# A written order for the loads at the entry of attention, and a fixed order for the first row norms, in a two-layer encoder on one Trainium2 core

## The chip, the cores and the metric

The kernel runs on one core of one Trainium2 chip. The metric is the device time of one execution in microseconds (us). The engines are named as in the profile: PE (TensorE, the matrix engine; PEld is its weight load), DVE (VectorE), ACT (ScalarE), POOL (GpSimd) and SP (SyncE, which here only issues loads and stores). SPq, ACTq and POOLq are the sequencers that issue for an engine.

## What is computed

Two layers of an encoder on x of 1024 rows by 1024 columns, all float32. The reference, cut to what matters here:

```python
for l in range(2):
    h = rms_norm(x, g_norm[l])
    z = h @ w_in[l]                      # 2656 columns: q, k, v, gate of A, B, C
    # A: 6 heads, 2 key heads, per-head norm of q and k, axial rotary, full attention
    oa = dense_gqa_blocks(qa, ka, va, HEAD_DIM ** -0.5) * silu(ag)
    # B: 6 heads, 2 key heads, window of 128, a sink logit per head
    ob = windowed_sink_gqa(qb, kb, vb, b_sink, HEAD_DIM ** -0.5) * silu(bg)
    # C: 4 heads, low-rank q and kv, a shared rotary key
    oc = mla_blocks(qc_nope, qc_rope, kc_nope, kc_rope, vc, 96 ** -0.5) * silu(cg)
    x = x + concat([oa, ob, oc], -1) @ w_out[l]
return rms_norm(x, final_g)
```

## The kernel before

Rows come in NS = 8 tiles of 128. A product of float32 accuracy is made of three matmuls on values split in a high and a low part (`mm3`: high by high, high by low, low by high), so nearly everything has an `h` and an `l` twin: `wh`/`wl` of a weight piece, `hTh`/`hTl` of the transposed normed rows.

A layer goes through these stages. **Norm and v** (layer 0): for each row tile x is loaded (`load_x`, up to XBUFS tiles ahead), normed (`stage.norm`: squares on ACT, `ms_x` on DVE, a power on POOL for `rs_x`, the product `xt` on DVE), transposed by PE (`stage.turn`, `pt`) and multiplied with the v columns (`v_rows`, `pzv`). The v weights are two pieces `wst_1`, `wst_2`, split by POOL (`wh`) and DVE (`wl`) as every weight piece after them. **q and k of A, B and C** (`pza`, `pzb`, `pzc`): the results are normed, rotated, split and written to DRAM (`d_qa`, `d_ka`, `d_qb`, `d_kb`, `d_qc`, `d_kn`, `d_k`, `d_vc`). **Gate** (`pg`): PE computes the gate columns, ACT makes `g` of each result, and each is written to DRAM (`d_gate`, 256 KB a write) by ACT's own queue; all other loads and stores are issued by SP. **Attention** sweeps eight query tiles `qt`. For each, A's units take scores `sa` from keys `ka` and stacked queries `qsta`, B's take `sb` from `kb` and `qstb`, C's take `sc` from `k` and `qc`; the softmaxed scores are transposed (`ppa`, `ppb`, `ppc`) and multiplied with v (`poa`, `pob`, `poc`; C's v is `vC`). `gta`, `gtb`, `gtc` are the gate values read back for a query tile. **Output** (`pw`): the result times w_out, plus x; in the last layer with the final norm.

The keys are two halves of precision: `ka` and `kb` are two tiles each (high and low), each loaded by two loads of 512 KB; a stack of queries is four loads of 96 KB. C's keys `k` are six loads (three of 512 KB, three of 256 KB), its queries `qc` of one query tile 15 loads of 64 KB or less, `vC` one load of 1 MB.

Two things set the order. A scheduler, which sees data, buffers and priorities, orders the instructions of each engine when the kernel is built; `tc.keep_in_program_order` pins an instruction to the order in which the code says it (class `Engine` does so for all engines while `pinned[0]` is set). And each engine takes its instructions strictly in that order, so an instruction that waits holds all behind it, on SP too. Each load or store signals its end on one of eight completion counters, DMAHW0 to DMAHW7, which SP's and ACT's loads and stores take in turn; a load or store waits until the one that had its counter last has ended. The waits that the order listing below shows at loads are these.

Of the kernel before, what the change touches and what calls it, by code (L numbers as in the profile page):

```python
# [8 lines left out]
F32 = mybir.dt.float32  # L9
F32R = mybir.dt.float32r  # L10
AF = mybir.ActivationFunctionType
ALU = mybir.AluOpType
# [4 lines left out]
EPS = 1e-6  # L17
# [17 lines left out]
XBUFS = 6  # L35
# [10 lines left out]
def kernel(  # L46
# [21 lines left out]
    nc = tc.nc  # L68
    P = 128
    S, D = x.shape[1], x.shape[2]  # L70
    DEPTH = norm_g.shape[0]
    NS = S // P
# [6 lines left out]
    dram = ctx.enter_context(tc.tile_pool(name="dram", bufs=1, space=DRAM))  # L79

    queue_behind = [None]
    last_pow = [None]

    def after(ins, first):
# [9 lines left out]
    def dma(dst, src, eng=None):  # L94

        a, b = (t.bitcast(F32) if t.dtype == F32R else t for t in (dst, src))
        ins = (eng or nc.sync).dma_start(a, b)  # L97
        if queue_behind[0] is not None and eng is None:
            after(ins.ins, queue_behind[0])
        return ins.ins  # L100

    pinned = [False]
# [123 lines left out]
    for l in range(DEPTH):  # L226
# [18 lines left out]
        with stage.ph as ph:  # L245
# [32 lines left out]
            if l == 0:  # L278
                stage.open_px()
                warm = ps_o("warm")  # L280
                for _ in range(WARM):
                    T.matmul(warm[:, 0:P], lhsT=ident, rhs=ident, start=True, stop=True)
                xts = {}

                def load_x(st):
                    xts[st] = stage.px.tile([P, D], F32, tag="xt", name=f"xt{l}_{st}", bufs=XBUFS)
                    queue_behind[0] = dma(xts[st], x_src[st * P : (st + 1) * P, :])

                load_x(0)
                dma(stage.ng, norm_g[l].partition_broadcast(P))  # L290
                stage.load_wv()
                for st in range(1, XBUFS):
                    load_x(st)
                for st in range(NS):
                    xt = xts[st]
                    junk = stage.px.tile([P, D], F32, tag="junk", name=f"jk{l}_{st}", bufs=1)
                    stage.norm(st, xt, xt, junk)
                    stage.turn(st, xt, ps_t)
                    if st + XBUFS < NS:
                        load_x(st + XBUFS)  # L300
                    if st:
                        v_rows(st - 1)
                v_rows(NS - 1)
                stage.px_.close()
            else:
                for st in range(NS):
                    v_rows(st)
                    if st == LATE:
                        stage.turn(NS - 1, stage.xt, ps_t)
                stage.px_.close()  # L310
# [344 lines left out]
        with ExitStack() as ph:  # L655
# [195 lines left out]


            if True:
                ks, start = {}, {}
                for g, m0 in (("a", 0), ("b", 3)):
                    start[g] = Gqa(g, 0, m0)
# [272 lines left out]
            def groups_c():  # L1129
                for hp in range(2):  # L1130
                    ks = KeysC(hp)
                    for q0 in range(0, NS, 3):
                        c = GroupC(ks, hp, q0)
                        if hp or q0:
                            c.gate()
                        else:

                            for it in (start["a"], start["b"], c):
                                it.gate()
                            yield None  # L1140
                        for par in range(2):
                            grp = {}
                            yield [UnitC(c, par, g, grp) for g in range(c.nq)]

            def units():

                cs = groups_c()
                next(cs)
                for qt in range(NS):
                    if qt == 0:  # L1150
                        a, b = start["a"], start["b"]
                    else:
                        a, b = Gqa("a", qt, 0), Gqa("b", qt, 3)
                        a.gate()
                        b.gate()
                    for kv in range(2):
                        grp = {}
                        for g in range(3):
                            yield UnitA(a, kv, g, grp)
                            if g == 1:  # L1160
                                yield UnitB(b, kv)
                        if 2 * qt + kv in C_AT:
                            yield from next(cs)
                first = True
                for us in cs:
                    for u in us:
                        yield u
                        if first:
                            yield ab_done
                            first = False  # L1170
# [8 lines left out]
        with ExitStack() as ph:  # L1179
# [10 lines left out]
            for st in range(NS):  # L1190
                nm = f"{l}_{st}"
                s_ = slice(st * P, (st + 1) * P)
                if st > 1:
                    x_row(st)
                    out_hl(0, 6, st)
                if st:
                    out_hl(6, 8, st)
                y = xrows[st]
                if last:
                    ss = small.tile([P, 2], F32, tag="ss2", name=f"ssf{nm}")  # L1200
                for c in range(2):
                    cs = slice(c * 512, (c + 1) * 512)
                    for _ in out_part(st, c, MW if (st, c) in wa_.ps else 0, 8):
                        pass
                    ps = wa_.ps[st, c]
                    V.tensor_add(y[:, cs], ps, y[:, cs])
                    if last:
                        jk = wb.tile([P, 512], F32, tag="jk", name=f"jkf{nm}_{c}", bufs=2)
                        A.activation(jk, y[:, cs], AF.Square, accum_out=ss[:, c : c + 1])
                if last:  # L1210
                    V.tensor_add(ss[:, 0:1], ss[:, 0:1], ss[:, 1:2])
                    r = rstd_of(ss[:, 0:1], D, f"f{nm}", 1)
                    for c in range(2):
                        cs = slice(c * 512, (c + 1) * 512)
                        V.tensor_mul(y[:, cs], y[:, cs], fg[:, cs])
                    A.activation(y[:, 0:512], y[:, 0:512], AF.Copy, scale=r[:, 0:1])
                    dma(x_dst[s_, 0:512], y[:, 0:512], nc.scalar)
                    V.tensor_scalar(y[:, 512:1024], y[:, 512:1024], r[:, 0:1], None, ALU.mult)
                    dma(x_dst[s_, 512:1024], y[:, 512:1024])
                    continue  # L1220
                dma(x_dst[s_, :], y)
                if not last:
                    xt = stage.px.tile([P, D], F32, tag="xt", name=f"xt{l + 1}_{st}", bufs=XTB)
                    stage.norm(st, xt, y, xt)
                    if st == WV_ST:
                        stage.load_wv()
                    if st < NS - 1:
                        stage.turn(st, xt, ps_t)
                    else:
                        stage.xt = xt  # L1230
# [72 lines left out]
```

## Time and profile before

| | |
|---|---|
| time, median of 3 runs | 1340.75 us (1340.05 to 1341.09) |
| the profiled execution, its own time | 1342.18 us |
| its span in the trace | 1340.4 us, mean granted clock of PE 0.988 |
| PE busy | 1301.9 us, 97% of the span |
| PEld, DVE, ACT, POOL busy | 85%, 67%, 54%, 39% |
| read and written in DRAM | 107.35 MB and 57.67 MB |

A share is the time in which the engine had an instruction at work, over the span. PE's 97% leaves 38.5 us in which it had none. The granted clock is that of PE, as a share of its full speed (2.4 GHz); 0.5 is its lower level, 1.2 GHz.

### The profile page before, as it was taken

Reading aid. Unit: us, or ns where it says so; the run is one execution under the profiler, and the core shown is the slowest. Engines: PE = TensorE matmul, PEld = TensorE weight load, DVE = VectorE, ACT = ScalarE, POOL = GpSimd, SP = SyncE. Lnnn points to the kernel's source line nnn. Section 1 sums busy time; section 2 is a strip of 40 time slices with the busy share of each in tenths; the row PEclk is TensorE's granted clock in tenths of the full one; section 3 lists DMA queues with packets and bytes.
Section 4 is the critical chain, followed back from the end, with each engine's and each line's share of the span. In section 5 each row is a group of like instructions: output and inputs, shape, how many; then the busy total and the mean of one; then the engine's idle time right before and its main releaser. Section 6 shows DMA issues by size and latency. Waiting matters only on the chain.

```text
span 1340.4 us, 21695 instructions
## 1 busy us (share of the span) xinstructions
PE 1301.9 (97%) x7320; PEld 1139.5 (85%) x7320; DVE 892.3 (67%) x2246; ACT 720.2 (54%) x1547; POOL 524.6 (39%) x602
## 2 busy tenths in 40 slices
PE   7999999989999999999999999999799999999997
PEld 7888998868989899888898889887698999998786
DVE  6685662057888988875537766600789899998543
ACT  4232341166888889842313324311688899897332
POOL 4330121025666676752023111300366766667100
PEclk8999999998999999999999999999899999999999
DMA  7234469353222432257323344783622225113443
GB/s 252 87 124 148 135 202 261 122 132 89 68 61 60 111 90 58 74 179 235 131 78 121 122 132 161 242 196 103 154 68 64 59 69 139 46 45 126 165 146 112
DMA packets 176878, 166.46 MB, mean 124 GB/s; under 512 B 22528, under 2 KB 149376, under 8 KB 176768
## 3 DMA queue, kind: packets, MB, share of 16 engines
q1 hardware_dynamic: 158016, 140.43, 36.5%
q10 hardware_dynamic: 18752, 24.65, 5.3%
q8 instruction: 58, 0.95, 0.3%
q14 instruction: 52, 0.43, 0.1%
HBM read 107.35 MB, written 57.67 MB: 123 GB/s over the span
## 4 chain that ended last, share of the span: by engine, by line
PE 82%; DVE 6%; DMA 5%; ACT 2%; issue 2%; SPq 2%; POOL 1%; POOLq 0%; DVEq 0%; ACTq 0%
PE pg L136 13%; PE pw L136 12%; PE pzb L114 7%; PE pza L114 7%; PE poa L136 6%; PE sc L136 5%; PE ppa L703 4%; PE pzc L136 4%; PE sa L136 4%; PE pzv L136 4%; PE ppc L703 3%; PE poc L136 3%; PE pob L136 2%; PE sb L136 2%; SPq L97 2%
## 5 line engine op out<-in xcount | busy, mean ns | idle before, releaser
L684 DVE CUSTOM_DVE_ANT_0 pa<-sa,zero 128x512 f32<-128x512 f32 x96 | 65.5, 682 | 136.6 <-PE sa L136 134.8
L711 POOL TENSOR_SCALAR ptha<-pfa 128x512 fp32r<-128x512 f32 x96 | 59.4, 621 | 206.7 <-ACT pfa L710 202.3
L712 POOL TENSOR_TENSOR ptla<-pfa,ptha 128x512 fp32r<-128x512 f32 x96 | 123.6, 1290 | 6.1
L136 PE MATMUL sa<-ka,qsta 128*128 128x512 f32 x384 | 121.3, 417 | 0.8 <-ACT g L617 0.7
L694 ACT ACTIVATE pa<-pa,nmxa 128x1024 f32<-128x1024 f32 x96 | 111.2, 1160 | 14.0 <-DVE nmxa L684 13.9
L136 PE MATMUL sc<-k,qc 128*128 128x512 f32 x384 | 111.5, 410 | 0.9 <-DVE nmxc L684 0.9
L703 PE MATMUL ppa<-ident,pa 128*128 128x128 f32 x768 | 106.3, 273 | 0.7 <-DVE ptlb L715 0.5
L703 PEld LDWEIGHTS ppa<-ident,pa 128*128 128x128 f32 x768 | 90.9, 141 | 14.8 <-DVE ptla L715 1.2
L136 PE MATMUL pw<-woh,oh 128*128 128x512 f32 x256 | 99.4, 394 | 2.1 <-ACT oh L1001 1.1
L136 PE MATMUL pw<-wol,oh 128*128 128x512 f32 x256 | 100.6, 394 | 0.8 <-DVE wol L1021 0.6
L136 PE MATMUL pg<-hTh,wh 128*128 128x512 f32 x256 | 100.3, 392 | 0.0
L136 PE MATMUL pg<-hTh,wl 128*128 128x512 f32 x256 | 100.2, 391 | 0.0
L136 PE MATMUL pg<-hTl,wh 128*128 128x512 f32 x256 | 100.1, 391 | 0.0
L136 PE MATMUL pw<-woh,ol 128*128 128x512 f32 x256 | 99.1, 393 | 0.3 <-DVE ol L1002 0.3
L216 POOL TENSOR_SCALAR wh<-wst 128x512 fp32r<-128x512 f32 (+1 forms) x64 | 39.6, 638 | 148.3 <-PE pzb L114 79.4
L617 ACT ACTIVATE g<-pg 128x512 f32<-128x512 f32 x32 | 19.1, 598 | 137.5 <-PE pg L136 90.5
L136 PE MATMUL poa<-ptha,vAB 128*128 128x384 f32 x256 | 89.4, 349 | 1.0 <-DVE ob L793 1.0
L136 PE MATMUL poa<-ptla,vAB 128*128 128x384 f32 x256 | 88.2, 344 | 0.0
L694 ACT ACTIVATE pc<-pc,nmxc 128x1024 f32<-128x1024 f32 x64 | 74.0, 1157 | 10.2 <-DVE nmxc L684 9.7
L136 PEld LDWEIGHTS sc<-k,qc 128*128 128x128 f32 x384 | 66.6, 189 | 10.7 <-DVE nmxc L684 2.0
L712 POOL TENSOR_TENSOR ptlc<-pfc,pthc 128x512 fp32r<-128x512 f32 x56 | 74.0, 1327 | 1.5
L684 DVE CUSTOM_DVE_ANT_0 pa<-sa,zero,nmxa 128x512 f32<-128x512 f32 x96 | 71.1, 743 | 4.5 <-PE sa L136 1.8
(217 smaller groups left out, 3817.3 us busy)
## 6 DMA issues: line engine op xcount, KB each, us to landing
wst<-in_w_in_dram SPq DMA_DIRECT2D x20, 512.0 KB, 3.6
d_gate<-g ACTq DMA_DIRECT2D x32, 256.0 KB, 2.4
wost<-in_w_out_dram SPq DMA_DIRECT2D x32, 256.0 KB, 2.9
wst<-in_w_in_dram SPq DMA_DIRECT2D x16, 384.0 KB, 4.4
qsta<-d_qa SPq DMA_DIRECT2D x64, 96.0 KB, 2.6
qstb<-d_qb SPq DMA_DIRECT2D x64, 96.0 KB, 2.6
k<-d_kn SPq DMA_DIRECT2D x12, 512.0 KB, 6.8
qc<-d_qc SPq DMA_DIRECT2D x96, 64.0 KB, 2.2
```

What stands on the lines that cost most here:

```text
L97: ins = (eng or nc.sync).dma_start(a, b)
L114: return lambda *a, **k: tc.keep_in_program_order(f(*a, **k))
L136: T.matmul(ps, lhsT=a, rhs=b, start=first and i == 0, stop=last and i == len(parts) - 1)
L216: G.tensor_scalar(h, f, 1.0, 0.0, ALU.mult, ALU.add)
L617: A.activation(g, ps, AF.Silu)
L684: V.tensor_tensor_reduce(p[:, c * 512 : (c + 1) * 512], ps, zero[:, 0:1].to_broadcast([P, 512]), -1.0, nmx[0][:, 0:1] if c else 3.0e38, AL ...
L694: A.activation(p, p, AF.Exp, scale=-1.0, bias=nmx[1][:, 0:1], accum_out=sm)
L703: T.transpose(pt[:, (j - q0) * P : (j - q0 + 1) * P], p[:, j * P : (j + 1) * P], ident)
L711: G.tensor_scalar(hi, f, 1.0, 0.0, ALU.mult, ALU.add)
L712: G.tensor_tensor(out=lo, in0=f, in1=hi.bitcast(F32), op=ALU.subtract)
```

## The change

In layer 0 the first norms, transposes and v products are pinned in the order of the code, and that order is new: tiles 0 and 1 are normed first, x of tile 1 is loaded between the two pieces of the v weights, and in the loop the norm of tile st+1 stands ahead of the transpose of tile st and the v product of tile st-1. In both layers SP's loads from the first `qsta` on are pinned in the order of the code until the first unit of C has been prepared (`in_order`); the query stacks and gate values of A and B for query tile 1 are now asked for ahead of C's first loads, and for later tiles in the second half of the tile before. In the final norm the first half's share of the mean and its product with the gain are made when the first half is there.

```diff
@@ dma @@
+        if in_order[0] and eng is None:
+            tc.keep_in_program_order(ins)
@@ layer 0, norm and v @@
+                pinned[0] = True
+                def normed(st):
+                    junk = stage.px.tile([P, D], F32, tag="junk", name=f"jk{l}_{st}", bufs=1)
+                    stage.norm(st, xts[st], xts[st], junk)
+                stage.wv = [], [], 256
+                steps = stage.w_steps(stage.wv, [(512, 128), (1536, 128)])
                 load_x(0)
                 dma(stage.ng, norm_g[l].partition_broadcast(P))
-                stage.load_wv()
-                for st in range(1, XBUFS):
+                normed(0)
+                next(steps)
+                stage.turn(0, xts[0], ps_t)
+                load_x(1)
+                normed(1)
+                next(steps)
+                for st in range(2, XBUFS):
                     load_x(st)
-                for st in range(NS):
-                    xt = xts[st]
-                    junk = stage.px.tile([P, D], F32, tag="junk", name=f"jk{l}_{st}", bufs=1)
-                    stage.norm(st, xt, xt, junk)
-                    stage.turn(st, xt, ps_t)
-                    if st + XBUFS < NS:
-                        load_x(st + XBUFS)
-                    if st:
-                        v_rows(st - 1)
+                for st in range(1, NS):
+                    if st < NS - 1:
+                        normed(st + 1)
+                    stage.turn(st, xts[st], ps_t)
+                    v_rows(st - 1)
+                    if st + XBUFS - 1 < NS:
+                        load_x(st + XBUFS - 1)
                 v_rows(NS - 1)
+                pinned[0] = False
@@ attention, its first loads @@
+                in_order[0] = True
                 ks, start = {}, {}
                 for g, m0 in (("a", 0), ("b", 3)):
                     start[g] = Gqa(g, 0, m0)
@@ groups_c @@
-                            for it in (start["a"], start["b"], c):
-                                it.gate()
+                            c.gate()
                             yield None
@@ units @@
+                a, b = start["a"], start["b"]
+                ahead = Gqa("a", 1, 0), Gqa("b", 1, 3)
+                a.gate()
+                b.gate()
                 cs = groups_c()
                 next(cs)
+                in_order[0] = False
                 for qt in range(NS):
-                    if qt == 0:
-                        a, b = start["a"], start["b"]
-                    else:
-                        a, b = Gqa("a", qt, 0), Gqa("b", qt, 3)
+                    if qt:
+                        a, b = ahead
                         a.gate()
                         b.gate()
                     for kv in range(2):
+                        if kv and 0 < qt < NS - 1:
+                            ahead = Gqa("a", qt + 1, 0), Gqa("b", qt + 1, 3)
@@ output, last layer @@
+                        if c == 0:
+                            e0 = small.tile([P, 1], F32, tag="e0", name=f"e0{nm}")
+                            V.tensor_scalar(e0, ss[:, 0:1], 1.0 / D, EPS, ALU.mult, ALU.add)
+                            V.tensor_mul(y[:, cs], y[:, cs], fg[:, cs])
                 if last:
-                    V.tensor_add(ss[:, 0:1], ss[:, 0:1], ss[:, 1:2])
-                    r = rstd_of(ss[:, 0:1], D, f"f{nm}", 1)
-                    for c in range(2):
-                        cs = slice(c * 512, (c + 1) * 512)
-                        V.tensor_mul(y[:, cs], y[:, cs], fg[:, cs])
+                    ms = small.tile([P, 1], F32, tag="ms1", name=f"ms_f{nm}")
+                    V.scalar_tensor_tensor(ms, ss[:, 1:2], 1.0 / D, e0, ALU.mult, ALU.add)
+                    r = small.tile([P, 1], F32, tag="rs1", name=f"rs_f{nm}")
+                    G.tensor_tensor(out=r, in0=ms, in1=mhalf[:, 0:1], op=ALU.pow)
+                    tc.keep_in_program_order(nc.vector.tensor_mul(y[:, 512:1024], y[:, 512:1024], fg[:, 512:1024]))
```

What the change moves is seen in the order of the built programs, which says nothing of times. Lines of the changed kernel lie 1 to 19 lower, and buffer numbers differ. A row gives line, operation, destination and source with buffer numbers, and shape; x4 is four such in a row.

The first place is SP at the entry of attention in layer 0; `waits` names the semaphores that a load waits for. Before, from A's low keys on:

```order
L97 DMA ka_0_2792<-d_ka_81 64x2x1024 [waits DMAHW2_49]
L97 DMA qstb_0_2795<-d_qb_79 64x3x128 [waits DMAHW3_49]
L97 DMA qstb_0_2795<-d_qb_79 64x3x128 [waits DMAHW4_49]
L97 DMA qstb_0_2795<-d_qb_79 64x3x128 [waits DMAHW5_49]
L97 DMA qstb_0_2795<-d_qb_79 64x3x128 [waits DMAHW7_49]
L97 DMA kb_0_2802<-d_kb_82 64x2x1024 [waits DMAHW0_49,PE_49]
L97 DMA kb_0_2802<-d_kb_82 64x2x1024 [waits DMAHW1_49]
L97 DMA kb_0_2805<-d_kb_82 64x2x1024 [waits DMAHW6_49,DMAHW2_49,Activation_49]
L97 DMA kb_0_2805<-d_kb_82 64x2x1024 [waits DMAHW3_49]
```

Now the same loads:

```order
L98 DMA ka_0_2792<-d_ka_81 64x2x1024 [waits DMAHW6_49]
L98 DMA qstb_0_2795<-d_qb_79 64x3x128 [waits DMAHW7_49]
L98 DMA qstb_0_2795<-d_qb_79 64x3x128 [waits DMAHW0_49]
L98 DMA qstb_0_2795<-d_qb_79 64x3x128 [waits DMAHW1_49]
L98 DMA qstb_0_2795<-d_qb_79 64x3x128 [waits DMAHW2_49]
L98 DMA kb_0_2802<-d_kb_82 64x2x1024 [waits DMAHW3_49,PE_49]
L98 DMA kb_0_2802<-d_kb_82 64x2x1024 [waits DMAHW4_49]
L98 DMA kb_0_2805<-d_kb_82 64x2x1024 [waits DMAHW5_49,Activation_49]
L98 DMA kb_0_2805<-d_kb_82 64x2x1024 [waits DMAHW6_49]
```

The loads stand in the same order, but their counters are others. Seven of ACT's gate writes of the changed program show from where the counters are counted on:

```order
L98 DMA d_gate_77<-g_1_0_2469 128x512 [waits DMAHW4_49,Activation_49]
L98 DMA d_gate_77<-g_2_0_2497 128x512 [waits DMAHW5_49,Activation_49]
L98 DMA d_gate_77<-g_0_1_2525 128x512 [waits DMAHW6_49,Activation_49]
L98 DMA d_gate_77<-g_1_1_2553 128x512 [waits DMAHW7_49,Activation_49]
L98 DMA d_gate_77<-g_2_1_2581 128x512 [waits DMAHW0_49,Activation_49]
L98 DMA d_gate_77<-g_3_0_2609 128x512 [waits Activation_49]
L98 DMA d_gate_77<-g_4_0_2637 128x512 [waits Activation_49]
```

In the changed program the gate writes from `g_0_1` on (in the order `g_0_1`, `g_1_1`, `g_2_1`, `g_3_0`, `g_4_0`, `g_5_0`, `g_3_1`, `g_4_1`) take counters 6, 7, 0, 1, 2, 3, 4, 5 and the last of the stage, `g_5_1`, takes 0; the four loads of `qsta_0` take 6, 7, 1, 2 and `ka` 3, 4, 5, 6. So the first load of `qsta` waits for the write of `g_0_1`, the first three loads of `ka` wait for those of `g_5_0`, `g_3_1` and `g_4_1`, and the second load of `qstb` for that of `g_5_1`. Before, these loads were counted on from the stores and weight loads of the stage ahead; the only gate write that one of them waits for is that of `g_6_1`, which is computed ahead of the nine above.

The second place is SP a little later. Before, from the last gate values of query tile 0 on, C's keys stand after one load of `qstb_1`, and the other three `qstb_1` loads stand 22 rows later, behind 15 loads of `qc`:

```order
L97 DMA gtc_0_0_2848<-d_gate_77 128x384
L97 DMA qsta_1_3133<-d_qa_78 64x3x128 [waits DVE_49,PE_49]
L97 DMA qsta_1_3133<-d_qa_78 64x3x128 [waits DMAHW6_49]
L97 DMA qsta_1_3133<-d_qa_78 64x3x128 [waits DMAHW7_49]
L97 DMA qsta_1_3133<-d_qa_78 64x3x128 [waits DMAHW0_49]
L97 DMA qstb_1_3140<-d_qb_79 64x3x128 [waits DMAHW1_49]
L97 DMA k_0_0_2814<-d_kn_83 64x2x1024 [waits DMAHW2_49,Activation_49]
```

Now `qstb_1` is loaded whole ahead of C's keys, and `vC`, which stood ahead of the gate values before, comes between C's keys and `qc`:

```order
L98 DMA qstb_1_2821<-d_qb_79 64x3x128 [waits DMAHW0_49]
L98 DMA gta_0_2828<-d_gate_77 128x3x128 [waits DMAHW1_49]
L98 DMA gtb_0_2830<-d_gate_77 128x3x128 [waits DMAHW2_49]
L98 DMA k_0_0_2832<-d_kn_83 64x2x1024 [waits DMAHW3_49,Activation_49]
L98 DMA k_0_0_2832<-d_kn_83 64x2x1024 [waits DMAHW4_49]
L98 DMA k_0_2812<-d_kn_83 64x2x1024 [waits DMAHW5_49]
L98 DMA k_0_2812<-d_k_84 64x1024 [waits DMAHW6_49]
L98 DMA k_0_2812<-d_k_84 64x1024 [waits DMAHW7_49]
L98 DMA k_0_2813<-d_k_84 64x1024 [waits DMAHW0_49]
L98 DMA vC_0_2833<-d_vc_85 128x8x256 [waits DMAHW1_49]
L98 DMA qc_0_0_2842<-d_qc_80 64x2x128 [waits DMAHW2_49]
```

The third place is POOL in the norm stage of layer 0: `rs_x` are the powers of the row norms, `wh` the high parts of the weight pieces, where `wst_3` and `wst_4` are the first of the stage after. Before, with the first factors of the rotary tables (`tabs`) behind the norms:

```order
L216 TENSOR_SCALAR wh_1_121<-wst_1_120 128x512 x2
L216 TENSOR_SCALAR wh_2_130<-wst_2_129 128x512 x2
L130 TENSOR_TENSOR rs_x_1_177<-ms_x_1_175,mhalf 128x1
L130 TENSOR_TENSOR rs_x_2_228<-ms_x_2_226,mhalf 128x1
L130 TENSOR_TENSOR rs_x_3_277<-ms_x_3_275,mhalf 128x1
L130 TENSOR_TENSOR rs_x_4_326<-ms_x_4_324,mhalf 128x1
L130 TENSOR_TENSOR rs_x_5_375<-ms_x_5_373,mhalf 128x1
```

Now:

```order
L117 TENSOR_SCALAR wh_1_129<-wst_1_128 128x512 x2
L117 TENSOR_TENSOR rs_x_1_158<-ms_x_1_156,mhalf 128x1
L117 TENSOR_SCALAR wh_2_162<-wst_2_161 128x512 x2
L117 TENSOR_TENSOR rs_x_2_183<-ms_x_2_181,mhalf 128x1
L117 TENSOR_TENSOR rs_x_3_234<-ms_x_3_232,mhalf 128x1
L219 TENSOR_SCALAR wh_3_555<-wst_3_554 128x512 x2
L219 TENSOR_SCALAR wh_4_563<-wst_4_562 128x512 x2
L117 TENSOR_TENSOR rs_x_4_285<-ms_x_4_283,mhalf 128x1
```

Tile 1's power is now ahead of the second weight piece, and the splitting of `wst_3` and `wst_4`, unpinned, has come ahead of tile 4's power. On PE the transpose `pt` of tile 1 now stands ahead of the first v product `pzv_0`; before it stood behind part of it.

## Rows read from the trace of the kernel before

**Rows 1.** Page: busy time of PE; chain that ended last, by engine.

```profile
PE 1301.9 (97%) x7320; PEld 1139.5 (85%) x7320; DVE 892.3 (67%) x2246; ACT 720.2 (54%) x1547; POOL 524.6 (39%) x602
...
PE 82%; DVE 6%; DMA 5%; ACT 2%; issue 2%; SPq 2%; POOL 1%; POOLq 0%; DVEq 0%; ACTq 0%
```

**Rows 2.** Busy time by stretch: length, engines, granted clock, DMA share, GB/s.

```profile
10.00:20.00 10.00, 7.36 (x42) 6.49 (x42) 7.74 (x13) 6.82 (x14) 4.31 (x6) 0.83 0.91 346
20.00:30.00 10.00, 8.83 (x62) 8.66 (x61) 9.28 (x17) 5.54 (x12) 5.29 (x8) 0.83 0.77 243
...
280.00:290.00 10.00, 9.49 (x53) 7.01 (x53) 9.43 (x37) 9.56 (x21) 3.05 (x4) 1.00 0.86 206
...
300.00:310.00 10.00, 6.31 (x23) 5.58 (x24) 4.98 (x14) 1.88 (x6) 1.49 (x2) 0.57 0.56 154
...
960.00:970.00 10.00, 8.90 (x34) 7.97 (x35) 5.88 (x18) 3.88 (x12) 1.48 (x2) 0.63 0.56 159
```

**Rows 3.** Timeline of PE: start, length, line, operation, [idle before, releaser].

```profile
303.45 0.98 PE L136 MATMUL sb<-kb,qstb 128*128 128x384 f32 x2 [6.50 <-DMA qstb<-d_qb]
...
311.56 0.62 PE L136 MATMUL sc<-k,qc 128*128 128x512 f32 x2
...
960.64 0.66 PE L136 MATMUL sb<-kb,qstb 128*128 128x384 f32 x1 [5.62 <-DMA qstb<-d_qb]
...
969.36 0.63 PE L136 MATMUL sc<-k,qc 128*128 128x512 f32 x2
```

**Rows 4.** Chain that ended last, both entries of attention: start, length, what.

```profile
279.48 2.34 DMA d_gate<-g
...
281.90 0.58 SPq L97
...
285.42 10.77 DMA k<-d_k
...
308.20 3.05 PE poa L136 x16
...
936.58 2.49 DMA d_gate<-g
...
942.53 10.93 DMA k<-d_k
```

**Rows 5.** Timeline of SP's issues: start, length, what is loaded.

```profile
219.73 0.58 SPq L97 DMA_DIRECT2D kb<-d_kb  x1
...
222.12 0.58 SPq L97 DMA_DIRECT2D kb<-d_kb  x1
...
286.06 14.86 SPq L97 DMA_DIRECT2D qc<-d_qc  x15
300.97 1.82 SPq L97 DMA_DIRECT2D qstb<-d_qb  x3
```

**Rows 6.** DMA issues at 212.48, 214.20 and 244.84: count, KB, us to landing.

```profile
ka<-d_ka SPq DMA_DIRECT2D x1, 512.0 KB, 4.7
...
d_gate<-g ACTq DMA_DIRECT2D x1, 256.0 KB, 9.8
...
vC<-d_vc SPq DMA_DIRECT2D x1, 1024.0 KB, 6.5
```

**Rows 7.** Start: timeline of PE and POOL, chain, issue of `wst_4` at 20.57.

```profile
8.90 1.09 PE L171 MATMUL pt<-ident,xt 128*128 128x128 f32 x8 [0.82 <-DVE xt L164]
...
33.41 1.20 POOL L216 TENSOR_SCALAR wh<-wst 128x512 fp32r<-128x512 f32 x2
...
47.37 2.75 PE pza L114 x12
...
wst<-in_w_in_dram SPq DMA_DIRECT2D x1, 512.0 KB, 10.1
```

**Rows 8.** The chain's last pieces.

```profile
1334.44 0.16 DVE ssf L1211
1334.60 0.60 DVE y L1215
```

More of the change, by code (lines that the diff above doesn't have):

```diff
@@ L81 @@
     queue_behind = [None]
+    in_order = [False]
     last_pow = [None]
```

## The prediction

> **What bounds the kernel now.** I read the page first: PE is busy 97% of the span and holds 82% of the chain that ended last [rows 1]. So the time is PE's work plus the 38.5 us in which PE has nothing (1340.4 less 1301.9), and a change that leaves PE's work alone can only move these. Next the busy time by stretch, to see where they lie [rows 2]: PE lacks 2.6 and 1.2 us in 10 to 30, and 3.7 us in 300 to 310, where it also runs at a granted clock of 0.57, which is nearly its lower level throughout; 960 to 970 shows 0.63. The timeline of PE names the two big holes [rows 3]: 6.50 us before 303.45 and 5.62 us before 960.64, both in B's scores `sb`, both ended by the load of `qstb`. These are the queries of tile 1, which stand on SP behind C's keys and 15 loads of `qc`: SP spends 286.06 to 300.92 on these and issues the last three `qstb` loads from 300.97 on [rows 5].
>
> The chain of waits tells why SP was late itself [rows 4]: the last gate write on ACT's queue, issued at 279.48, took 2.34 us, and only at 281.90 did SP issue C's first key load, though the gate's values are no data of that load. Its completion counter is the one that the gate write had. That is the mechanism on which the forecast rests, and the chain shows it again at 285.42, where a `qc` load waits 10.77 us for a key load whose counter it gets. SP's timeline shows it for `kb`: two of its loads are issued at 219.73 and 222.12 [rows 5], 2.4 us apart though an issue takes 0.6, as the `ka` loads that had their counters land one by one. So 512 KB take 2.4 us when loads follow one another.
>
> **The start.** PE transposes tile 1 ahead of `pzv_0`. In the trace PE starts tile 0's transposes at 8.90 [rows 7] after 0.82 of waiting, and lacks 2.64 and 1.17 more in 10 to 30 [rows 2]: 4.6 us of holes. Tile 1's x now comes between the weight pieces (I put its landing at about 9.9), and behind it stand square, `ms_x`, power and product, so that `xt` of tile 1 is there at about 14.5: PE waits some 4.5 us in one piece, then works at the lower clock for 2 to 3 us. Next, POOL now splits `wst_3` and `wst_4` ahead of tile 4's power. `wst_4` was issued at 20.57 and took 10.1 us; it is about 1.5 us earlier now, so lands at 29.1. Behind it come 1.20 for `wh` [rows 7], the power, and DVE's product behind the two `wl`, which makes tile 4 ready at about 32.3, while PE has run out of work at about 27.7: 4.6 us more. Against these 9.1 stand the 4.6 that vanish with the old order. The first `pza` comes at about 52 in place of 47.37. I take +4.5; the bounds are -2 (tile 4 isn't waited for, and some of the old holes close) and +6.5 (both holes and more of the lower clock).
>
> **The entry of attention.** The edit's intention can be read from the order: `qstb_1` goes ahead of C's keys. But the pinned loads have been given counters behind those of the gate writes (front part, first place). Before, the `ka` and `kb` loads were issued between 212 and 226, under the gate's matmuls, and cost PE nothing. Now the third `ka` load (first of the low keys) waits for the write of `g_4_1`, at about 276, and the second `qstb_0` load for that of `g_5_1`, the last thing of the gate stage. So `kb` can't be issued before the gate stage is over, and PE has nothing else in its queue: eight `sa`, then `sb`.
>
> Layer 0, step by step. The last gate write is issued at 279.48. It takes 2.34 us where little else moves [rows 4] and took 9.8 where four `ka` loads were under way [rows 6]. Two low-key loads will be under way, of which the second lands at about 282.8. I put its end at 283.5 (bounds 281.8 and 289.3). Three `qstb` issues of 0.65 follow (the 0.58 of the row and the step to the next), so `kb` is issued from 285.5 on. Its first load lands 4.7 later, as the first `ka` load did [rows 6], the others 2.4 apart: 290.2, 292.6, 295.0, 297.4. PE, done with the gate at about 279, waits some 3.5 us for the low `ka`, then from about 284.4 to 292.6 for the high `kb`, and once more, 1 to 3 us, for the low one.
>
> Now what is late next. The last loads of `qsta_1` and the first two of `qstb_1` wait for the `kb` loads' counters, up to 297.4; two more `qstb_1`, `gta` and `gtb` bring SP to 300.6 for C's first key load. In the trace, C's keys took from 281.90 to 296.19 (285.42 and 10.77 [rows 4]), 14.3 us. So they are in at 314.9. Behind them on the same queue is now the 1 MB of `vC`, by the pace above 4.8 us more, then the first `qc`: 320.0. Before, `sc` started at 311.56 [rows 3], with 16 `poa` (3.05 [rows 4]) and two short transposes already done that now stand behind it; that place is 308.2. So PE is 11.8 us behind. More waiting means more time at the lower clock: in 300 to 310 PE worked 6.31 us at a mean clock of 0.57 [rows 2], so some 4.5 to 5 us at the half, of which 2.2 to 2.5 are lost; two or three holes in place of one add about one such price, a little less where the work goes on. I take 2.0, in all **+13.8**.
>
> Layer 1 in the same way: gate write issued at 936.58 [rows 4], ended at 940.6, `kb` from 942.5 to 954.5, C's first key load at 957.7, its keys in 14.3 later (939.14 to 942.53 and 10.93 before [rows 4]), `vC` 4.8, `qc` 0.3: 977.2. `sc` stood at 969.36 [rows 3], less the same 3.4: 966.0. With 2.0 for the clock **+13.2**.
>
> The bounds of an entry: if `vC` doesn't hold `qc` up and the gate write ends as it did, PE waits for `kb` alone: 3.5 and about 7, less the 6.5 of the hole that is gone, with 2 for the clock: +6. If the gate write takes 6 us longer, and both further holes cost their clock: +18 to +22.
>
> On the queues: the write of 9.8 us stood on ACT's queue, the `ka` loads on SP's, and the write landed only when those issued before it had [rows 6]. The Trainium skill, page "DMA: Bandwidth & Descriptors", section "Queues, rings and completion order", says that a DMA engine takes turns between the rows it has work for, a packet at a time; by that the last gate write, alone in its row, would have ended well before four times its size on SP's row, and now at about 282 in place of 283.5. The row speaks for the later end; the sum would be 1.5 less for a layer by the rule.
>
> **Other edits.** Pairs of A and B for later tiles are built in the second half of a tile: the same loads, a few us earlier, beside PE work that has no holes there; nothing, and if the scheduler puts one behind a long wait, below 1 us. At the end `ssf` (0.16) and one `y` product (0.60) [rows 8] leave the chain, which then goes on to the power as before: **-0.7** (bounds -0.4 and -1.4).
>
> **Sum.** 4.5 + 13.8 + 13.2 - 0.7 = 30.8. The profiled execution took 1342.18, 1.43 over the median of the runs; the added waits are the same for both: 1373.0 for a profiled one, 1371.5 by the median, forecast 1371.
>
> **Rivals.** (a) Faster: the gate writes' ends come as early as `ka` and `kb` are needed, so that only the order of `qstb_1` counts. PE then loses neither the 6.5 and 5.6 us of holes nor the 2.2 of half clock behind each: -16.5 for both, -12.7 with start and end: 1328. It decides at PE's first `sb`, at about 280.7: the high `kb` must have landed by then. The order's waits speak against it, the chain's wait at 281.90 too; for it, only that the semaphores of the built program might be met in another way than I read. Chance 0.05.
> (b) The hole only moves: `ka` and `kb` are hidden, and `sc` waits where `sb` did, since `vC` is now ahead of `qc`. Then 2 to 3.5 us less per layer and 4.5 more at the start: within 2.7 us (0.2%) of before, which is about what a measurement of this kernel can tell from no change. Chance 0.04.
> (c) The loads go faster than C's keys went: 346 GB/s is seen in 10 to 20, 206 in 280 to 290 [rows 2]. At the higher rate `kb` needs 1.5 us a load, C's keys and `vC` are in at about 308, and PE waits for `kb` alone: +6 a layer, 1340.75 + 12 + 4.5 - 0.7 = 1356.6. Against it, the 206 was seen with the queue full, for these same tensors. With the start gaining 2 it is 1350. Chance of 1350 to 1361: 0.16.
> The page named above, section "Anatomy of one DMA", gives 2.0 us and the bytes over 436 GB/s for a load; by an estimate from that, 512 KB take 1.2 us each in a row, and (c) would hold. The rows' 2.4 us decide against it.
> (d) Everything piles up behind the gate write: 1382 to 1390. Chance 0.08. What is left below 1350 and still slower: 0.03.
>
> The forecast's own case, 1361 to 1382, keeps 0.64. The range reaches into (c) and a little into (d): 1351 to 1383. Faster 0.05, same 0.04, slower 0.91.
>
> **What would show it.** SP issues `kb` behind 283; its `qstb_0` waits for `d_gate`. PE has holes before `sa` and `sb` at the entry, ended by loads of `ka` and `kb`, and one before `sc`, ended by `qc`; the clock between 280 and 325 is low in more than one stretch. At the start the first `pza` comes at about 52, with holes before `pt` of tiles 1 and 4. The forecast is wrong if `kb` is there before 281, or if `sc` doesn't wait.

## The result and the profile after

The changed kernel takes 1379.31 us (median of 4 runs, 1378.79 to 1380.94); the kernel before 1340.42 (4 runs, 1340.05 to 1341.09). The ratio is 1.0292, interval 1.0274 to 1.0309: slower by 39 us. Forecast were 1371 and a range of 1351 to 1383. The two profiled executions lie 36.6 us apart (spans of 1377.0 and 1340.4): that of the changed kernel was the fastest of its four, that of before lay above its median. The stages below are worked out from these two.

The page of the changed kernel, the rows that answer to [rows 1]:

```profile
span 1377.0 us, 21709 instructions
PE 1305.5 (95%) x7320; PEld 1141.6 (83%) x7320; DVE 887.9 (64%) x2246; ACT 719.1 (52%) x1547; POOL 523.7 (38%) x602
...
PE 79%; DMA 8%; DVE 4%; ACT 4%; issue 3%; SPq 1%; POOL 1%; POOLq 0%; ACTq 0%; DVEq 0%
```

PE does the same 7320 matmuls in nearly the same busy time, but has nothing in 71.5 us, not 38.5, and DMA is 8% of the chain that ended last, not 5%. Where these 33 us are is read from the timeline of PE, at the first matmuls of stages and at holes:

```profile
14.79 1.97 PE L117 MATMUL pt<-ident,xt 128*128 128x128 f32 x8 [4.68 <-DVE xt L117]
...
34.04 1.94 PE L117 MATMUL pt<-ident,xt 128*128 128x128 f32 x8 [5.17 <-DVE xt L117]
...
55.54 0.40 PE L117 MATMUL pza<-wh,hTh 128*128 128x512 f32 x1
...
291.64 2.67 PE L139 MATMUL sa<-ka,qsta 128*128 128x512 f32 x5 [3.96 <-DMA ka<-d_ka]
302.24 0.98 PE L139 MATMUL sb<-kb,qstb 128*128 128x256 f32 x3 [7.93 <-DMA kb<-d_kb]
...
329.37 1.62 PE L139 MATMUL sc<-k,qc 128*128 128x512 f32 x3 [6.26 <-DMA qc<-d_qc]
...
726.76 0.40 PE L117 MATMUL pza<-wh,hTh 128*128 128x512 f32 x1
...
973.70 0.98 PE L139 MATMUL sb<-kb,qstb 128*128 128x256 f32 x3 [8.25 <-issue]
...
1000.52 1.62 PE L139 MATMUL sc<-k,qc 128*128 128x512 f32 x3 [6.05 <-DMA qc<-d_qc]
...
1369.85 0.39 PE L139 MATMUL pw<-woh,ol 128*128 128x512 f32 x1
```

Before, the first `pza`, that of layer 1 and the last `pw` stood here:

```profile
47.20 0.40 PE L114 MATMUL pza<-wh,hTh 128*128 128x512 f32 x1
...
703.94 0.40 PE L114 MATMUL pza<-wh,hTh 128*128 128x512 f32 x1
...
1332.53 0.39 PE L136 MATMUL pw<-woh,ol 128*128 128x512 f32 x1
```

These three places are the marks of the stages, here and below. So the start costs 8.3 us, the rest of layer 0 14.5 (22.8 less 8.3), layer 1 14.5 (37.3 less 22.8), and the end gives 0.7 back (7.15 from the last `pw` to the end, 7.87 before). The sum is 36.6.

The busy time by stretch (length, PE, PEld, DVE, ACT, POOL, granted clock, DMA share, GB/s), beside [rows 2]:

```profile
10.00:20.00 10.00, 5.32 (x31) 5.21 (x30) 8.23 (x12) 4.15 (x8) 3.28 (x5) 0.66 0.94 343
...
30.00:40.00 10.00, 5.96 (x31) 5.99 (x32) 7.12 (x12) 1.50 (x4) 2.70 (x4) 0.66 0.42 117
...
290.00:300.00 10.00, 2.67 (x5) 1.23 (x5) 2.74 (x8) 2.37 (x4) 0.00 (x0) 0.59 0.73 169
300.00:310.00 10.00, 6.24 (x28) 5.04 (x28) 3.06 (x11) 2.15 (x4) 3.76 (x4) 0.73 1.00 206
...
320.00:330.00 10.00, 3.74 (x19) 2.71 (x18) 6.31 (x19) 7.11 (x19) 4.21 (x5) 0.79 0.92 202
330.00:340.00 10.00, 9.53 (x53) 8.54 (x52) 4.75 (x14) 4.78 (x11) 2.13 (x4) 0.86 0.56 155
```

In or at the end of each of the large holes the granted clock falls to its lower level (0.50), and it stays there for some us after PE has taken up work again. Two numbers are counted for a stage in stretches of 1 us: the holes, as what PE's busy time lacks to 1 us, and the cost of the clock, as the busy time multiplied by what the granted clock lacks to 1. The second is an estimate, which takes all of PE's work as slowed in proportion. At the entry in layer 0 holes and clock come to 7.7 and 2.5 us before, 20.5 and 4.4 after; in layer 1 7.6 and 3.1, then 19.4 and 4.9; at the start 4.6 and 3.2, then 12.3 and 4.5.

SP's timeline at the entry (columns as in [rows 5]):

```profile
273.39 12.07 SPq L98 DMA_DIRECT2D ka<-d_ka  x4
285.51 8.57 SPq L98 DMA_DIRECT2D qstb<-d_qb  x4
294.18 2.56 SPq L98 DMA_DIRECT2D kb<-d_kb  x4
...
309.91 1.89 SPq L98 DMA_DIRECT2D k<-d_kn  x3
...
314.59 0.59 SPq L98 DMA_DIRECT2D vC<-d_vc  x1
```

And what SP waited for from 240 to 330 (total, times, longest):

```profile
SPq L98 <- DMA d_gate<-g: 70.3, 8, 29.6
```

Before, `kb` was issued from 219.73 on [rows 5], in the gate stage; now from 294.18, behind it. SP spends 70.3 us in eight waits for gate writes, whose data none of these loads reads. The Trainium skill (page "DMA: Bandwidth & Descriptors", section "Anatomy of one DMA") says that a wait is served by the sequencer that issues and not by the DMA engines. The trace agrees, since one wait of 29.6 us stops every load behind it.

The last gate write, issued at 287.66, in the view of DMA issues (KB, us to landing):

```profile
d_gate<-g ACTq DMA_DIRECT2D x1, 256.0 KB, 4.6
```

And in the chain that ended last the second low `ka` load and the last `kb` load:

```profile
284.86 6.65 DMA ka<-d_ka
...
296.13 10.67 DMA kb<-d_kb
```

The write ends at 292.24, behind the `ka` load (291.51); `qstb` and `kb` wait for it, and the last `kb` is in at 306.80. In layer 1 the last gate write took 4.6 us too. There the trace names no releaser for the hole before `sb` (`issue` in the row at 973.70), but the second `kb` load landed at about 973.5, 0.2 us ahead of it.

### The profile page after: what moved, and what is told of

Its sections match the earlier page's. It is cut to its first block, busy times and chain, and to the rows that moved or that the text cites. A ratio compares the mean times of both kernels' runs of the same rounds, so it can differ in the third digit from the quotient of the medians.

```text
span 1377.0 us, 21709 instructions
## 1 busy us (share of the span) xinstructions
PE 1305.5 (95%) x7320; PEld 1141.6 (83%) x7320; DVE 887.9 (64%) x2246; ACT 719.1 (52%) x1547; POOL 523.7 (38%) x602
## 4 chain that ended last, share of the span: by engine, by line
PE 79%; DMA 8%; DVE 4%; ACT 4%; issue 3%; SPq 1%; POOL 1%; POOLq 0%; ACTq 0%; DVEq 0%
PE pg L139 12%; PE pw L139 11%; PE pzb L117 6%; PE pza L117 6%; PE poa L139 6%; PE sc L139 5%; PE ppa L718 5%; PE pzc L139 4%; PE sa L139 4%; PE ppc L718 3%; PE poc L139 3%; PE pob L139 2%; PE pzv L139 2%; PE ppb L718 2%; PE sb L139 2%
## 5 line engine op out<-in xcount | busy, mean ns | idle before, releaser
L139 PE MATMUL sc<-k,qc 128*128 128x512 f32 x384 | 113.1, 414 | 13.2 <-DMA qc<-d_qc 12.3
L219 POOL TENSOR_SCALAR wh<-wst 128x384 fp32r<-128x384 f32 (+1 forms) x60 | 35.9, 617 | 147.2 <-PE pzb L117 79.2
L139 PEld LDWEIGHTS sa<-ka,qsta 128*128 128x128 f32 x384 | 65.2, 191 | 22.4 <-issue 7.7
L730 DVE TENSOR_TENSOR ptla<-ppa,ptha 128x512 fp32r<-128x512 f32 x96 | 65.2, 684 | 27.8 <-ACT ptha L729 25.1
```

Source lines behind the costliest of these rows:

```text
L139: T.matmul(ps, lhsT=a, rhs=b, start=first and i == 0, stop=last and i == len(parts) - 1)
L219: G.tensor_scalar(h, f, 1.0, 0.0, ALU.mult, ALU.add)
L730: V.tensor_sub(lo, ptv, hi.bitcast(F32))
```

## The experiments

The kernel before ran beside each group of runs on the same chip; ratios are to it. Its medians were 1342.56, 1343.47 and 1341.91 in the three groups.

**entry**: the parts `dma`, attention, `groups_c` and `units` of the diff alone; start and end as before.

> Only the part at the entry of attention (the pinned written order of the loads and the earlier stacks of query tile 1); start and end as before. Theory of the completion counters: each entry costs what the trace of the changed kernel shows, 14.6 and 14.8 us, whatever the start does, so 1340.4 + 29.4 = 1370, with kb issued behind the last gate write. Rival, the loss at an entry is partly an after-effect of the late start: clearly less, below 1362.

Measured 1376.99, ratio 1.0258 (1.0244 to 1.0272). The mechanism is there without the start:

```profile
282.19 2.78 PE L139 MATMUL sa<-ka,qsta 128*128 128x512 f32 x5 [3.86 <-DMA ka<-d_ka]
293.46 0.98 PE L139 MATMUL sb<-kb,qstb 128*128 128x256 f32 x3 [8.49 <-DMA kb<-d_kb]
...
320.85 1.62 PE L139 MATMUL sc<-k,qc 128*128 128x512 f32 x3 [5.96 <-DMA qc<-d_qc]
```

The holes are those of the whole change within 0.6 us, and the rival falls. But the loss is 5 us over the expected 29.4: after the holes PE ran longer at half clock. Worked out as above, the clock took 6.7 and 5.7 us at the two entries, where it took 4.4 and 4.9 in the whole change: 3 of the 5. The other 2 are not accounted for.

**entry_gpool**: the same, with the gate writes issued by another queue.

```diff
-                            dma(d_gate[:, m0 + m, hf * 512 : (hf + 1) * 512], g, nc.scalar)
+                            dma(d_gate[:, m0 + m, hf * 512 : (hf + 1) * 512], g, nc.gpsimd)
```

> The entry part as in the run entry, pin and order unchanged, but the gate writes are issued by POOL's queue in place of ACT's, and so take other completion counters. Theory of the counters: the pinned loads of ka and kb then wait only for stores and loads of the stage ahead, land before 245, and no hole stands before sa and sb; what is left is sc waiting for qc behind vC, some 5 us, in place of the holes of before, so about 1334 (1328 to 1341). Rival, the pin and the order of PE that came with it cost the time themselves: 1360 or more. Rival, loads pinned behind the gate are late for another reason than the counters: the same.

Measured 1337.66, ratio 0.9965 (0.9953 to 0.9978). SP's timeline:

```profile
210.73 2.66 SPq L98 DMA_DIRECT2D ka<-d_ka  x4
...
218.75 7.46 SPq L98 DMA_DIRECT2D kb<-d_kb  x4
```

PE's only longer wait from 270 to 335:

```profile
PE sc L139 <- DMA qc<-d_qc: 3.8, 1, 3.8
```

The order of the loads on SP and the pin are those of the run entry; with other counters for the gate writes `kb` is issued in the gate stage again and 2.9% of the time is gone. From 235 to 325 SP has no wait for a gate write left, where the run entry has 70.0 us of them. That settles the cause: not the order as written, but the counters that the pinned loads share with the gate writes.

**ahead_no_pin**: the same part without its pin.

```diff
-        if in_order[0] and eng is None:
-            tc.keep_in_program_order(ins)
```

> The entry part without the pin: the code asks for the stacks of query tile 1 ahead of C's loads, but the scheduler places the loads. In the built order ka and kb then have the counters of before, and qstb of tile 1 stands whole ahead of C's keys. Theory: as in the run entry_gpool, kb early, no hole at sb, a hole of some 5 us at sc behind vC: about 1334 (1328 to 1341). Rival (the hole only moves): 1338 to 1342. Rival, the new order of asking costs by itself: 1355 or more.

Measured 1339.77, ratio 0.9978 (0.9960 to 0.9996): `ka` and `kb` early again, `qstb` of tile 1 ahead of C's keys, and the hole now at `sc`, in PE's waits at both entries:

```profile
PE sc L137 <- DMA qc<-d_qc: 4.5, 1, 4.5
...
PE sc L137 <- DMA qc<-d_qc: 3.7, 1, 3.7
```

And the busy time by stretch, with the granted clock third from the end:

```profile
300.00:310.00 10.00, 6.09 (x26) 5.93 (x27) 4.61 (x13) 4.34 (x14) 1.48 (x2) 0.83 0.57 138
960.00:970.00 10.00, 8.66 (x36) 7.99 (x37) 3.97 (x10) 3.19 (x9) 1.48 (x2) 0.66 0.45 128
```

The gain is smaller than expected. In the trace the hole moves to `sc` and the half clock comes with it (1.7 and 2.8 us, where it was 2.5 and 3.1); the rival that the hole only moves is near the truth. The ten runs spread from 1334.56 to 1344.41, and the trace is of one of 1341.46; what the others lose is not seen.

**tail**: the edit of the final norm alone.

> Only the final norm's edit. Theory: the add (0.16) and one product (0.60) leave the last chain: 1339.7, with the last power 0.7 earlier against the last pw. Rival, the pinned product delays the copy of the other half: 1340.4 or more.

Measured 1342.39, ratio 1.0002 (0.9989 to 1.0014): too small for the runs. From the last `pw` to the end the trace has 7.47 us, 7.87 before; but the nine traces without this edit have between 7.47 and 7.94, and the four with it between 7.15 and 7.50. The means differ by 0.35, and what one pair of traces differs by is no measure of the edit.

**start**: the part at the start of layer 0 alone.

> Only the part at the start of layer 0 (pinned order, tile 1's x between the v weights); the entries and the end as before. Theory: the first pza comes 8.3 us later, as in the changed kernel, and nothing behind it gives that back: ratio 1.006, about 1349. Rival, from the runs so far (the entry part alone came out only some 2 to 3 us below the whole change): the start's loss is made up by what follows, ratio 1.002 or less.

Measured 1353.96, ratio 1.0082 (1.0063 to 1.0100). The first `pza` comes at 55.39, 8.2 us later, and the 8.2 are still there at the first `sa`; the rival falls. The trace is of a run of 1351.21, 2.8 us below the median; where the others lose that is not shown. PE's waits from 8 to 60 name the work that is late:

```profile
PE pt L114 <- DVE xt L114: 12.0, 5, 5.3
```

**start_behind**: start, with the first weight pieces of the next stage pinned behind the norms.

```diff
+            pinned[0] = True
             ws = load_w([(0, 512)])
+            pinned[0] = False
```

> The start part, but the splitting of the first two weight pieces of the next stage is pinned behind the norms on POOL and DVE. Theory: the hole before tile 4's transposes (5.17 us in the changed kernel) comes from POOL waiting for wst_4 ahead of tile 4's power; it shrinks below 1 us with the half clock behind it, first pza at 49 to 51 in place of 55.5, ratio 1.002. Rival, tile 4 is late by its own load and norm: the hole stays, ratio 1.006.

Measured 1359.04, ratio 1.0123 (1.0105 to 1.0142). The hole before tile 4 is gone and the first `pza` stands at 47.51, earlier than expected, but the theory missed what is late next: the pieces behind `wst_3` and `wst_4` get their buffers only when these two are split. POOL has made the high parts by 42.4, but DVE makes the low parts (`wl`) behind its last `vAB`, from 48.46 on; only then is the next piece issued, and `pza` waits for it, the longest time here. From the chain and from PE's timeline:

```profile
48.46 1.29 DVE wl L114 x2
...
49.77 3.54 DMA wst<-in_w_in_dram
...
54.13 0.54 PE L114 MATMUL pza<-wh,hTh 128*128 128x512 f32 x1 [2.12 <-POOL wh L114]
```

At the last `pza` the loss is 8.0 us again; the same pin in layer 1 adds 6.4. Where the split of these pieces stands, ahead of tile 4's power or behind the norms, is a choice between two holes once the pin holds the norms.

**start_swap**: start, with the v product ahead of the transposes.

```diff
-                    stage.turn(st, xts[st], ps_t)
                     v_rows(st - 1)
+                    stage.turn(st, xts[st], ps_t)
```

> The start part with its pin, but in the loop the v product of tile st-1 is pinned ahead of the transposes of tile st. Theory: part of the first hole (5.3 us before tile 1's transposes) is filled by the first half of pzv of tile 0, whose second half still waits for the second weight piece behind tile 1's power; POOL now has the next stage's weights behind tile 4's power and ahead of tile 5's, so the second hole moves to tile 5 and is shorter: first pza at 50 to 53, ratio 1.003 to 1.005. Rival, the holes are set by POOL's and DVE's order alone: first pza at 55, ratio 1.008.

Measured 1357.34, ratio 1.0114 (1.0098 to 1.0130): a miss of both. The first hole shrinks to pieces of 0.6 to 1.3 us, but each v product now waits for the split of the transposes right ahead of it, and a hole of 4.11 stands at 35.98, so the first `pza` comes at 59.22. With the pin, transposes ahead of the v product are the better order of the two.

**start_no_pin**: start without its pin.

```diff
-                pinned[0] = True
```

> The start part without the pin: the loads and norms are asked for in the new order, tile 1's x between the v weights, but the scheduler orders the engines, and puts pzv of tile 0 whole ahead of tile 1's transposes and the second weight piece ahead of tile 1's power. Theory: the loss of the start comes of the pinned order, so the first pza comes at 45.5 to 48.5 and the ratio is 0.998 to 1.002. Rival, the place of tile 1's x costs by itself, as it puts the second weight piece back: first pza behind 50, ratio 1.003 or more.

Measured 1352.36, ratio 1.0076 (1.0057 to 1.0095). The first `pza` is at 46.68, as the theory has it, 0.5 us ahead of before and 8.7 us ahead of the run start. Part of that is the clock, which stayed at 1.00 here; the last run below shows what is left for the pin. And 12.9 us are lost in one other place, the output stage of layer 0 (5 are won elsewhere, most of them in layer 1). PE's waits there:

```profile
PE pw L136 <- ACT oh L1011: 9.6, 2, 7.5
```

And SP's issues of the `ol` loads, from which `oh` is made:

```profile
593.72 4.07 SPq L97 DMA_DIRECT2D ol<-d_o  x2
...
618.71 1.00 SPq L97 DMA_DIRECT2D ol<-d_o  x2
```

The chain there runs over these loads of `ol`, the second behind six loads of `wst` that the scheduler put ahead of it. The edit touches nothing in that stage; the scheduler, given another start, placed them so. Why is not shown.

**pin_v_last**: entry with its pin, `vC` loaded behind `qc`.

```diff
-                    dma(self.v, d_vc[:, :, 2 * hp : 2 * hp + 2, :])
+                    self.load_v = lambda: dma(self.v, d_vc[:, :, 2 * hp : 2 * hp + 2, :])
...
                         c = GroupC(ks, hp, q0)
+                        if q0 == 0:
+                            ks.load_v()
```

> The entry part with its pin, but vC is loaded behind the 15 qc loads. Theory: of the hole before sc (6 us a layer) the 4.8 that vC takes on the queue vanish, and the holes before sa and sb stay (4 and 8.5): 3 to 5 us less a layer than the run entry, ratio 1.018 to 1.020. Rival, qc is late for C's keys alone and vC shares the queue without delaying it: as the run entry, 1.026.

Measured 1365.74, ratio 1.0174 (1.0144 to 1.0203), as expected: PE's waits at the entry of layer 0 keep the two that the gate writes cause, and the one at `sc` for `qc` is gone there (0.8 us in layer 1):

```profile
PE sb L139 <- DMA kb<-d_kb: 8.6, 2, 7.6
PE sa L139 <- DMA ka<-d_ka: 4.1, 1, 4.1
```

So `vC` ahead of `qc` is worth some 0.8% of the 2.6%, and the waits for the gate writes most of the rest.

**no_pin_v_last_tail**: ahead_no_pin, with `vC` behind `qc` as above and the edit of the final norm.

> The entry part without the pin, vC behind the qc loads, and the edit of the final norm: the version that the runs so far point to. Theory: ka and kb are early, qstb is ahead of C's keys, and without vC ahead of it qc comes with C's keys at about 299.5, so the last hole (4.5 and 3.7 us in the run ahead_no_pin, with some 1.7 to 3 us of half clock behind) falls to 0 to 1.5: ratio 0.988 to 0.992. Rival, C's keys are late themselves, so the hole stays: 0.997. Rival, vC is now late for poc: a new hole there, 0.997 or more.

Measured 1328.39 (1327.34 to 1329.69), ratio 0.9893 (0.9878 to 0.9907): faster than both kernels, 14 us less than before. PE's busy time on the page:

```profile
PE 1297.9 (98%) x7320; PEld 1129.9 (85%) x7320; DVE 887.4 (67%) x2246; ACT 719.2 (54%) x1547; POOL 529.2 (40%) x602
```

Two stretches at the entry of layer 0, beside [rows 2]:

```profile
290.00:300.00 10.00, 9.01 (x48) 6.50 (x47) 9.78 (x33) 9.60 (x26) 6.32 (x8) 1.00 0.62 141
300.00:310.00 10.00, 10.00 (x66) 9.16 (x66) 8.43 (x24) 8.79 (x18) 6.04 (x7) 1.00 0.94 238
```

And SP's issues there:

```profile
284.93 15.23 SPq L98 DMA_DIRECT2D qc<-d_qc  x15
300.20 0.55 SPq L98 DMA_DIRECT2D vC<-d_vc  x1
```

The hole at `sb` of before and the one at `sc` are gone, the clock stays at 1.00, and `vC`, issued at 300.20, delays nothing at the entry. There 1.5 and 2.5 us of holes are left, and nothing is lost to the clock: 8.6 and 8.3 us less than before by the count above. By the marks less of it stays: layer 0 behind the start is 3.2 us shorter, layer 1 7.5, the end 0.4. The output stage of layer 0 is 1.7 us longer; where the rest goes is not shown. And 2.9 of the 13.9 us between the two traces lie at the start, whose text is that of before: the holes there are the same (4.5 and 4.6 us), but the half clock took 3.2 us before and nothing here.

**no_pin_all**: that, with the start of start_no_pin.

> The whole change without any of its pins, with vC behind the qc loads. Theory: as the run no_pin_v_last_tail, whose two entries have no hole left, and with the start's order of asking worth at most 1 us either way: ratio 0.988 to 0.991. Rival, tile 1's x between the weights costs: 0.993 or more.

Measured 1332.89, ratio 0.9927 (0.9907 to 0.9946): between theory and rival. The entries are as in the run before it (PE is busy in 28.62 of the 30 us from 280 on). Its first `pza` comes at 49.83, in start_no_pin with the same text at 46.68; the first `pza` of seven runs with the start of before lies between 44.35 and 47.82. Much of that spread is the clock. Counted as above from 8 us to the first `pza`, the half clock took 4.8 us in this run and nothing in start_no_pin, with 6.0 and 6.3 us of holes. Kernels with the start of before have 4.0 to 4.6 us of holes, and two of them match in the clock: no_pin_v_last_tail (nothing lost, `pza` at 44.35) and tail (4.8 lost, at 47.82). Against these the new start without its pin is 2.3 and 2.0 us late, so its order costs some 2 us by itself. The run start, with 4.6 lost to the clock, has 12.1 us of holes and its `pza` 5.6 us behind that of this run: most of the 8.2 is the pin's.

## Why the prediction was right

**The mechanism and its place.** Right for the entries, and shown, not only argued: the entry part alone gives their loss, and other counters for the gate writes take it away with pin and order kept. The steps of layer 0, each with the 8.2 us that the start had added taken off: `kb` issued from 286.0 (forecast 285.5), its last load in at 298.6 (297.4), C's first key load issued at 301.7 (300.6), `sc` at 321.2 (320.0). The holes are 3.96, 7.93 and 6.26, where 3.5, 8.2 and the wait for `qc` were forecast.

**The gate write between two bounds.** It was put at 4 us, and took 4.6; with little else moving, the write before it (issued at 282.22) took 2.0. The row of 9.8 us [rows 6] spoke for a late end, and a late end came. What each queue moved from the issue of the last write at 287.66 to 290.5, and from there to 291.75 (packets, MB, share of 16 engines; q1 is SP's queue, q10 ACT's):

```profile
q1 hardware_dynamic: 257, 0.58, 102.7%
...
q10 hardware_dynamic: 144, 0.26, 70.0%
q1 hardware_dynamic: 108, 0.05, 21.3%
```

The write's 256 KB moved only when SP's loads under way were nearly done. The Trainium skill (page "DMA: Bandwidth & Descriptors", section "Queues, rings and completion order") says that a DMA engine takes turns between the queue rows that it has work for. The trace shows no such turns for this write, and in the trace of before the write issued at 214.20 did move beside SP's loads, but only from 218 on. Whether the engines had its work already while they moved SP's loads, the trace doesn't say.

**The two entries.** 13.8 and 13.2 were forecast, 14.5 each measured (with all that follows to the next mark). The clock's share was taken as 2.0 and came out as 2.0 and 1.8; the holes grew by 12.8 and 11.8.

**The start, the term that was off.** 4.5 was forecast, 8.3 measured, and that is the larger part of what the forecast lacks. Both holes were placed rightly and sized nearly so (4.5 and 4.6, measured 4.68 and 5.17). The step that failed is "Against these 9.1 stand the 4.6 that vanish": three smaller waits for `xt` remained (0.88, 0.67 and 0.83), so the holes grew by 7.7 and not 4.5, and the half clock behind them, named there, was not in the sum (it took 1.3 us more than before). The 8.3 lie above the stated bound of +6.5. That the time still fell into the range is owed to the room that the range left. Of the 8 us between forecast and result the start makes 3.8 and the entries 2.0; the rest is that the traced executions lie 36.6 us apart and the medians 38.9.

**The end.** -0.7 forecast, -0.7 in the trace of the change and -0.4 in that of tail; as the other traces spread by 0.5 without the edit, this agreement is in part luck.

**The rivals.** The faster one's condition was not met, and another kernel shows its price: without pin and with `vC` behind, the entries give 8.6 and 8.3 back by the count, where 16.5 was put for both, but only 3.2 and 7.5 of that are left at the ends of the layers. The hole that only moves is what ahead_no_pin shows (from the rival's own terms, the end included, it is 0.2 to 3.2 us less than before, not within 2.7). Faster loads did not come: the four `kb` loads were issued within 2.6 us and took until 306.80, 12.6 us from the first issue. Rival (d), from 1382 on, stayed out by 3 us, and what was longer than forecast was the start more than the wait for the gate write.

## What to carry to other kernels

A load that was pinned late in the order here got the completion counters of what was scheduled just ahead of it, even on another engine's queue; so look up, for each pinned load, whose end it waits for, and not only whose data. Where the scheduler already had the loads early, ask for them in the better order and leave the placing to it: order and later `vC` were worth 1.1% here (a part of it, in the trace, the clock at the start), the pin cost 2.8%. And count with a hole the half clock that follows it, and for each wait removed the transfer that is late next.

## What was not expected of the hardware

The same hole cost more or less by the clock alone. Behind the hole of 6 us at `sc` the whole change lost 1.7 us to the half clock in layer 0 and 2.3 in layer 1, the run entry 2.7 and 2.2; summed over an entry that made 4.4 and 6.7 in layer 0, with the same holes. The granted clock of the run entry in 320 to 330 was 0.69, with PE busy 9.14 us, that of the whole change 0.86 in 330 to 340. At the start of seven kernels with the same text, with holes of 4.0 to 4.6 us, the half clock took between nothing and 4.8 us, and the first `pza` moved by 3.5 us. What sets the length of the stretch at half clock is not shown.

And an edit at the start put 12.9 us into a stage some 550 us later (start_no_pin), through the scheduler alone; in the twelve other traces that stage, from the first `pw` of layer 0 to the first `pza` of layer 1, takes between 129.9 and 135.1 us, there 143.5: two kernels that differ in one place can differ in time somewhere else, and only a comparison stage by stage shows it.
